# The keys' second parts in two zero-filled tiles, and the first gate's tile kept in DRAM meanwhile

## The chip, the core and the metric

The kernel runs on one NeuronCore of a Trainium2 chip. The metric is the device time of one execution in microseconds (us), lower is better. Before the change the median of three runs is 1441.95 us (1440.77 to 1442.16). About 0.2%, some 2.9 us, is what a measurement of this kernel can tell from no change.

## What is computed

One layer of a decoder block on 1024 tokens of width 1024, all in float32, with a first half (short convolution beside attention) and a gated MLP. The change lies in the attention's scores and in one of the gates. Cut to these:

```python
u = rmsnorm(x, norm_mix_w)
cb, cc, cx, q, k, v, g_conv, g_attn = split(u @ w_in + b_in)
q, k = rope(q), rope(k)            # 8 query heads, 2 key heads, 64 wide
# blocks of 128 queries against 256 keys: the block before and its own
scores = einsum('bnqhgd,bnkhd->bnhgqk', qb, kk) * 64 ** -0.5
probs  = softmax(scores with a window of 128 and a sink per head)
y_attn = (probs @ v) @ w_attn_out + b_attn_out
merged = sigmoid(g_conv) * y_conv + sigmoid(g_attn) * y_attn
```

## The kernel before

Products have float32 accuracy by splitting: a factor a is held as a first part `ah` (float32 rounded to the matmul's own type, fp32r) and a second part `al = a - ah`, and a product is the sum of three matmuls, `ah bh + ah bl + al bh` (`mm3`, lines 144 to 146). `split` (lines 138 and 139) makes the parts: a copy on ScalarE (ACT), then a subtraction on VectorE (DVE).

A head is 64 wide, half of the 128 rows that TensorE (PE) contracts over. So for each of the two key heads g the kernel packs both query parts into one 128-row operand: `qs[g]` holds the first parts of the queries in the head's own 64 rows (`own[g]`) and their second parts in the other 64 (`other[g]`). `ks[g]` holds the keys' first parts in both halves. One matmul of `qs[g]` with `ks[g]` over 128 rows (line 444) therefore gives two of the three products. The third one, first parts of the queries by second parts of the keys, is a matmul over the 64 rows `own[g]` alone (line 445), with `kl`: one tile, in which head 0 has the upper 64 rows and head 1 the lower.

The work is in 16 steps (`Step`, line 432), one for each pair of a query block n and a head g. The order on PE, ACT and DVE is written out by hand (`tc.manual_schedule`, lines 514 to 561). In step i, PE does the scores of step i+1 (8 matmuls of 256 columns, alternating lines 444 and 445), the eight transposes `pt` of step i's probabilities (line 473, `turn`), half of a gate's or conv input's projection (`fill_part`: 24 matmuls of 512 columns, lines 144 to 146, with `w_fill` as weights), and step i's product with the values (4 matmuls `o`, line 483). DVE takes the masked maximum of the new scores (line 451, `maxima`), sums head halves, makes the second part `pl` of the transposed probabilities, stores the step before, normalises (line 467, `norms`) and, in every second step, makes the second part of the next `w_fill` (line 139). ACT does the exponentials, the first parts and the evictions (`fill_evict`, line 430). Scores of step 0 stand in front of the loop, between the two halves of fill 1.

The fills 0 to 7 are the projections `g_attn`; they stay in SBUF as `gas = filled[:8]` (line 562) until the attention's output is projected. There, the sigmoid of each (line 789) multiplies the output projection `ya` (line 795), and POOL's queue writes the result to DRAM (`msp`, line 796). All these tiles, and `ks`, `kl`, `vs`, the probabilities' parts and the raw weights `rin` of the next stage, are taken from one pool, `act`, of 16 tiles of 128x1024 float32. A new tile waits until the one that held its place is no longer read.

Outside the hand-written stretches a scheduler sets the order: so in the transition behind the loop, where `raw_ao` and `rin` are loaded by SP's queue (lines 121 and 601), which issues strictly in order. The next stage's first parts (`pin`, line 627) and the last store of the loop (`qs`, line 138) then stand in one queue on ACT.

Of the kernel before, what the change touches and what calls it, by code (L numbers as in the profile page):

```python
# [9 lines left out]
F32 = mybir.dt.float32  # L10
F32R = mybir.dt.float32r
I32 = mybir.dt.int32
AF = mybir.ActivationFunctionType
ALU = mybir.AluOpType

P = 128
D = 1024
T = 1024
# [17 lines left out]
COL_BIN = 0  # L36
# [36 lines left out]
def hybrid_kernel(ctx, tc, x, pos, cst, pcol, norms, w_in, w_ao, w_co, w_mix, w_up, w_down, out):  # L73
    nc = tc.nc
# [6 lines left out]
    dram = ctx.enter_context(tc.tile_pool(name="dram", bufs=1, space=bass.MemoryType.DRAM))  # L81
# [9 lines left out]
    def act(name, dt=F32, shape=(P, T)):  # L91
        return actp.tile(list(shape), dt, name=name, tag="act")
# [4 lines left out]
    def mid(name, dt=F32, shape=(P, 4, T)):  # L97
        return midp.tile(list(shape), dt, name=name, tag="mid")

    def ps(name, shape=(P, T)):  # L100
        return psum.tile(list(shape), F32, name=name, tag="mm")
# [8 lines left out]
    def pc(i):  # L110
        return pcol_sb[:, i:i + 1]
# [12 lines left out]
    def split_unit(raw, name, spare=False, eng=None):  # L124
        if spare:
            hi, lo = act(f"wh_{name}", F32R), act(f"wl_{name}", F32R)
        else:
            hl = wp.tile([P, 2, 1024], F32R, name=f"w_{name}", tag="w")
            hi, lo = hl[:, 0], hl[:, 1]
        split(raw, hi, lo, eng)  # L130
        return hi, lo
# [4 lines left out]
    def split(src, hi, lo, eng=None):  # L136

        first = nc.scalar.copy(hi, src)
        (eng or nc.vector).tensor_sub(lo, src, hi.bitcast(F32))
        return first  # L140
# [46 lines left out]
    def gemm_part(acc, w, u, cols, kcs=range(KC)):  # L187
        for kc in kcs:
            f = slice(kc * P, (kc + 1) * P)
            mm3(acc[:, cols], w[0][:, f], w[1][:, f], u[:, 0, kc, cols], u[:, 1, kc, cols], kc == 0, kc == KC - 1)  # L190
# [177 lines left out]
    def rope(part):  # L368
        r, sw, name = part
        q = tmp(f"q_{name}")  # L370
        nc.vector.tensor_mul(q, r, cos)
        nc.vector.tensor_mul(sw, sw, sin)
        nc.vector.tensor_add(q, q, sw)
        return q
# [3 lines left out]
    own = [slice(0, HD), slice(HD, P)]  # L378
    other = [own[1], own[0]]
    qs = [mid(f"qs{g}", F32R) for g in range(2)]  # L380
    ks = [act(f"ks{g}", F32R) for g in range(2)]
    kl = act("kl", F32R)

    def rope_keys(part):
        k = rope(part)
        for g in range(2):
            split(k[own[g]], ks[g][own[g]], kl[own[g]])
        for g in range(2):
            nc.vector.tensor_copy(ks[g][other[g]], ks[g][own[g]].bitcast(F32))

# [8 lines left out]
    cos, sin = table_cos, table_sin  # L399
    ps_q2 = gemm_feat(w_q2, u, "q2")  # L400
    rope_keys(turn["k"])
    turn[2] = rope_load(ps_q2, COL_BIN + U_Q + 2, "q2")
    for i in range(2):
# [12 lines left out]
    filled = [None] * len(fillers)  # L416
    w_fill, ps_fill = {}, {}
# [4 lines left out]
    def fill_part(f, h, kcs):  # L422
        if h == 0 and kcs[0] == 0:
            ps_fill[f] = ps(f"ps_fill{f}")
        gemm_part(ps_fill[f], w_fill[f], u, halves[h], kcs)

    def fill_evict(f):
        col, alloc = fillers[f]
        filled[f] = alloc(f"fill{f}")
        return nc.scalar.activation(filled[f], ps_fill[f], AF.Identity, bias=pc(COL_BIN + col))  # L430

    class Step:
        def __init__(self, i):
# [2 lines left out]
            self.queries = slice(self.n * P, (self.n + 1) * P)  # L436

        def scores(self):
            rows, g = own[self.g], self.g
            w0 = max(0, self.n - 1) * P  # L440
            kc = slice(w0, w0 + 256)
            self.s = ps(f"s{self.name}", (P, 4, 256))
            for c in range(4):
                nc.tensor.matmul(self.s[:, c], qs[g][:, c, self.queries], ks[g][:, kc], start=True, stop=False)
                nc.tensor.matmul(self.s[:, c], qs[g][rows, c, self.queries], kl[rows, kc], start=False, stop=True)  # L445

        def maxima(self):
            self.p = tmp(f"p{self.name}", F32, (P, 4, 256))
# [65 lines left out]
    with tc.manual_schedule(engines={mybir.EngineType.PE, mybir.EngineType.Activation, mybir.EngineType.DVE}):  # L514
        st = [Step(i) for i in range(len(steps))]
        fill_part(1, 0, range(KC))
        st[0].scores()
        fill_evict(0)
        st[0].maxima()
        fill_part(1, 1, range(KC))  # L520
# [3 lines left out]
        for i, step in enumerate(st):  # L524
            nxt = st[i + 1] if i + 1 < len(st) else None
            prev = st[i - 1] if i else None
            f, h = 2 + i // 2, i % 2
# [4 lines left out]
            if h == 0:  # L532
                fill_evict(f - 1)
# [26 lines left out]
        after_attention = st[-1].store().ins  # L560
        wa.append(split_unit(raw_ao[1], "ao1"))
    gas = filled[:8]

# [210 lines left out]
    for q in range(4):  # L776
# [9 lines left out]
        for jj in range(2):  # L786
# [4 lines left out]
            for cols in halves:  # L791
                for c in range(4):
                    f = slice((jj * 4 + c) * P, (jj * 4 + c + 1) * P)
# [417 lines left out]
    with tc.manual_schedule(engines={mybir.EngineType.PE, mybir.EngineType.Activation, mybir.EngineType.DVE, mybir.EngineType.SP}):  # L1211
# [9 lines left out]
        for i in range(4):  # L1221
# [7 lines left out]
            else:  # L1229
                rows = slice(3 * P, 4 * P)  # L1230
# [89 lines left out]
```

## Time and profile before

| what | us |
|---|---|
| median of three runs | 1441.95 |
| the profiled execution | 1441.58 |
| its span, first to last instruction | 1439.8 |
| PE busy, share of the span | 1418.2 (98%) |
| DVE busy | 1003.6 (70%) |
| ACT busy | 562.5 (39%) |
| POOL busy | 85.7 (6%) |
| mean granted clock of TensorE | 0.997 of 2.4 GHz |

Busy time of PE is the time in which at least one matmul is in the array; matmuls overlap, so their durations don't add up to it, and the distance from one start to the next (the pitch) is what counts. PEld is the loading of a matmul's weights, which can overlap the matmul ahead. An idle time is followed in brackets by what ended it. The chain of work that ended last is followed back from the last instruction, each piece with the time that it adds.

### The profile page before, as it was taken

The page shows a single profiled execution, that of the slowest core. Times are in us where ns is not written, and L with a number is a line of the kernel's source. Part 1 is how long each engine was busy: PE and PEld are TensorE (multiplying, and loading weights), DVE is VectorE, ACT ScalarE, POOL GpSimd, SP SyncE. Part 2 cuts the span into 40 slices and gives each one's busy share as a digit, 9 for nine tenths or more (in the row PEclk, how much of TensorE's full clock was granted, in tenths as well). Part 3 has the DMA queues.
Part 4 walks back from the last instruction along what each step waited for, and adds up shares of the span by engine and source line. Part 5 has one row for each costly group of instructions (what it writes and reads, how often), then busy time and mean ns, then how long its engine had stood idle before and what let it go on. Part 6 is the DMA issues. An engine that isn't in the chain of part 4 may idle for free.

```text
span 1439.8 us, 17099 instructions
## 1 busy us (share of the span) xinstructions
PE 1418.2 (98%) x6447; PEld 1164.9 (81%) x6447; DVE 1003.6 (70%) x1511; ACT 562.5 (39%) x897; POOL 85.7 (6%) x144
## 2 busy tenths in 40 slices
PE   8999999999999999999999999999999999999997
PEld 6987777788888888877888878888888888888886
DVE  7575676856788787545644697787777777655567
ACT  5545555623333333232323543333333334444343
POOL 5210000000000000000000000000000000000000
PEclk9999999999999999999999999999999999999999
DMA  5320000242455554255552222222232225797603
GB/s 217 89 59 30 30 16 30 88 161 74 161 205 205 191 185 178 76 177 196 184 174 103 74 98 107 101 105 95 88 110 93 99 94 197 275 377 256 195 31 146
DMA packets 68450, 193.18 MB, mean 134 GB/s; under 512 B 8144, under 2 KB 8400, under 8 KB 68368
## 3 DMA queue, kind: packets, MB, share of 16 engines
q1 hardware_dynamic: 53280, 139.64, 28.8%
q0 software_dynamic: 14368, 51.13, 9.2%
q10 hardware_dynamic: 720, 1.33, 0.3%
q8 instruction: 50, 0.82, 0.2%
q14 instruction: 32, 0.26, 0.1%
HBM read 136.75 MB, written 52.69 MB: 132 GB/s over the span
## 4 chain that ended last, share of the span: by engine, by line
PE 86%; DVE 6%; DMA 5%; ACT 2%; issue 1%; SPq 0%; DVEq 0%; ACTq 0%
PE xup L649 8%; PE zup L649 8%; PE yup L649 8%; PE dna L1151 8%; PE dnb L1151 6%; PE yin L649 5%; PE xin L649 5%; PE zin L649 5%; PE wup L649 4%; PE win L649 3%; PE ps_fill L144 3%; PE ps_fill L146 3%; PE ps_fill L145 3%; PE mx L145 2%; PE mx L146 2%; PE mx L144 2%
## 5 line engine op out<-in xcount | busy, mean ns | idle before, releaser
L1138 DVE TENSOR_TENSOR pd<-rd,pd 128x1024 fp32r<-128x1024 f32 x77 | 93.7, 1222 | 54.1 <-ACT pd L1141 50.3
L627 ACT CAST pup<-sup 128x512 fp32r<-128x512 f32 x80 | 47.8, 620 | 203.2 <-DVE sup L613 203.2
L1141 ACT CAST pd<-rd 128x1024 fp32r<-128x1024 f32 x77 | 80.6, 1053 | 104.1 <-PE dnb L1151 37.1
L1151 PE MATMUL dna<-pd 128*128 128x512 f32 x528 | 120.3, 389 | 0.0
L1151 PEld LDWEIGHTS dna<-pd 128*128 128x128 f32 x528 | 99.1, 188 | 20.5
L1151 PE MATMUL dnb<-pd 128*128 128x512 f32 x396 | 90.2, 389 | 0.0
L1151 PEld LDWEIGHTS dnb<-pd 128*128 128x128 f32 x396 | 74.3, 188 | 15.4
L649 PE MATMUL zin<-u,pin 128*128 128x512 f32 x360 | 86.1, 389 | 0.0
L627 ACT CAST pin<-sin 128x512 fp32r<-128x512 f32 x52 | 31.1, 620 | 135.3 <-DVE sin L613 126.4
L649 PEld LDWEIGHTS zin<-u,pin 128*128 128x128 f32 x360 | 67.6, 188 | 14.0
L630 DVE TENSOR_TENSOR pup<-sup,pup 128x512 fp32r<-128x512 f32 x80 | 53.6, 689 | 18.5 <-ACT pup L627 15.0
L144 PE MATMUL ps_fill<-u,w_fill 128*128 128x512 f32 x160 | 64.0, 400 | 0.0
L146 PE MATMUL ps_fill<-u,w_fill 128*128 128x512 f32 x160 | 62.5, 391 | 0.0
L145 PE MATMUL ps_fill<-u,w_fill 128*128 128x512 f32 x160 | 62.3, 389 | 0.0
L649 PE MATMUL yup<-b22h,pup 128*128 128x512 f32 x176 | 57.9, 390 | 0.9 <-DVE aup L665 0.9
L649 PE MATMUL zup<-b11h,pup 128*128 128x512 f32 x176 | 57.8, 390 | 0.0
L649 PE MATMUL zup<-b21h,pup 128*128 128x512 f32 x176 | 57.7, 389 | 0.0
L451 DVE CUSTOM_DVE_ANT_0 p<-s,cst_sb,pcol_sb 128x256 f32<-128x256 f32 x64 | 27.2, 480 | 37.2 <-PE s L445 34.6
L649 PE MATMUL yup<-bt1h,pup 128*128 128x512 f32 x160 | 52.5, 389 | 0.0
L649 PE MATMUL wup<-bt2h,pup 128*128 128x512 f32 x160 | 52.5, 389 | 0.0
L649 PE MATMUL xup<-bt3h,pup 128*128 128x512 f32 x160 | 52.5, 389 | 0.0
L649 PE MATMUL xup<-bt4h,pup 128*128 128x512 f32 x160 | 52.5, 389 | 0.0
(361 smaller groups left out, 3470.4 us busy)
## 6 DMA issues: line engine op xcount, KB each, us to landing
rup<-in_w_up SPq DMA_DIRECT2D x44, 512.0 KB, 3.5
rin<-in_w_in SPq DMA_DIRECT2D x30, 512.0 KB, 6.7
td<-in_w_down SPq DMA_DIRECT2D x22, 512.0 KB, 5.3
tsp<-td POOLq DMA_DIRECT2D x22, 512.0 KB, 3.7
rd<-tsp SPq DMA_DIRECT2D x44, 256.0 KB, 5.3
rd<-in_w_down SPq DMA_DIRECT2D x33, 256.0 KB, 5.3
rd<-hs SPq DMA_DIRECT2D x33, 256.0 KB, 3.7
x<-in_x SPq DMA_DIRECT2D x16, 512.0 KB, 3.7
```

What stands on the lines that cost most here:

```text
L144: nc.tensor.matmul(dst, ah, bh, start=first, stop=False)
L145: nc.tensor.matmul(dst, ah, bl, start=False, stop=False)
L146: nc.tensor.matmul(dst, al, bh, start=False, stop=last)
L451: nc.vector.tensor_tensor_reduce(out=self.p[:, c], in0=self.s[:, c], in1=masks[0 if self.n == 0 else 1], scale=SCALE, scalar=pc(COL_SINK + ...
L627: nc.scalar.copy(self.parts[p, q][:, 0], src())
L630: v.tensor_sub(t[:, 1], src(), t[:, 0].bitcast(F32))
L649: nc.tensor.matmul(dst, a, b[:, kc], start=first and i == 0, stop=last and i == 2, skip_group_check=p >= PLAIN and more)
L1138: v.tensor_sub(t[:, 2:], raws_d[n - 1], t[:, :2].bitcast(F32))
L1141: nc.scalar.copy(parts_d[n][:, :2], raws_d[n])
L1151: nc.tensor.matmul(sets[side, i], t[:, s, tok], t[:, b], start=g == 0 and k == 0 and not more, stop=g == NG - 1 and k == 2, skip_group_che ...
```

## The change

The keys' second parts get a tile for each head, `kl[0]` and `kl[1]`. The half that doesn't belong to the head is set to zero by two memsets on POOL. The second matmul of each pair contracts over all 128 rows: the rows of the queries' second parts meet zeros, and the sum stays what it was.

The pool `act` still has 16 tiles, so one is given back: fill 0 is written to DRAM (`gsp0`) by POOL's queue as soon as it is evicted, its place is free, and it is loaded again as `ga0` behind the loop by SP's queue.

```diff
-    kl = act("kl", F32R)
+    kl = [act(f"kl{g}", F32R) for g in range(2)]
+    for g in range(2):
+        nc.gpsimd.memset(kl[g][other[g]].bitcast(F32), 0.0)
...
-            split(k[own[g]], ks[g][own[g]], kl[own[g]])
+            split(k[own[g]], ks[g][own[g]], kl[g][own[g]])
...
+    gsp0 = dram.tile([P, T], F32, name="gsp0")
+
     def fill_evict(f):
         col, alloc = fillers[f]
         filled[f] = alloc(f"fill{f}")
-        return nc.scalar.activation(filled[f], ps_fill[f], AF.Identity, bias=pc(COL_BIN + col))
+        nc.scalar.activation(filled[f], ps_fill[f], AF.Identity, bias=pc(COL_BIN + col))
+        if f == 0:
+            nc.gpsimd.dma_start(gsp0, filled[f])
...
         def scores(self):
-            rows, g = own[self.g], self.g
+            g = self.g
...
-                nc.tensor.matmul(self.s[:, c], qs[g][rows, c, self.queries], kl[rows, kc], start=False, stop=True)
+                nc.tensor.matmul(self.s[:, c], qs[g][:, c, self.queries], kl[g][:, kc], start=False, stop=True)
...
     gas = filled[:8]
+    gas[0] = act("ga0")
+    nc.sync.dma_start(gas[0], gsp0)
```

Lines of the changed kernel behind the last edit are 10 higher (line 601 is 611, line 795 is 805). PE's instructions stand in the same order as before.

SP's queue, behind the loop: `raw_ao` are weights of the output projection, `rin` of the next stage. Before:

```order
L121 DMA raw_ao1_2159<-in_w_ao 128x1024
L121 DMA raw_ao2_2420<-in_w_ao 128x1024
L601 DMA rin00_2506<-in_w_in 128x1024
L601 DMA rin01_2507<-in_w_in 128x1024
L121 DMA raw_ao3_2493<-in_w_ao 128x1024
```

And now:

```order
L121 DMA raw_ao1_2164<-in_w_ao 128x1024
L121 DMA raw_ao2_2427<-in_w_ao 128x1024
L572 DMA ga0_2305<-gsp0_948 128x1024
L611 DMA rin00_2513<-in_w_in 128x1024
L611 DMA rin01_2514<-in_w_in 128x1024
L121 DMA raw_ao3_2500<-in_w_ao 128x1024
```

The reload of the first gate stands between the third `raw_ao` and the two first `rin`.

DVE in the same place, at the products of the output projection `ya` with the gates; `ta`, `tb` and `tc` are sums for the next stage. Before:

```order
L741 TENSOR_TENSOR tb0_2429<-u1_94 128x1024
L795 SCALAR_TENSOR_TENSOR fill0_1056<-ya0_2309,pcol_sb_89,fill0_1056 128x1024
L742 TENSOR_TENSOR ta0_2425<-ta0_2425,tb0_2429 128x1024
L139 TENSOR_TENSOR w_ao2_2422<-raw_ao2_2420,w_ao2_2422 128x1024
L795 SCALAR_TENSOR_TENSOR fill1_1114<-ya1_2337,pcol_sb_89,fill1_1114 128x1024
L741 TENSOR_TENSOR tb1_2433<-u1_94 128x1024
L630 TENSOR_TENSOR pin02_2513<-rin01_2507,pin02_2513 128x512
```

And now:

```order
L751 TENSOR_TENSOR tb0_2436<-u1_94 128x1024
L752 TENSOR_TENSOR ta0_2432<-ta0_2432,tb0_2436 128x1024
L139 TENSOR_TENSOR w_ao2_2429<-raw_ao2_2427,w_ao2_2429 128x1024
L751 TENSOR_TENSOR tb1_2440<-u1_94 128x1024
L805 SCALAR_TENSOR_TENSOR ga0_2305<-ya0_2316,pcol_sb_89,ga0_2305 128x1024
L752 TENSOR_TENSOR ta1_2433<-ta1_2433,tb1_2440 128x1024
L805 SCALAR_TENSOR_TENSOR fill1_1119<-ya1_2344,pcol_sb_89,fill1_1119 128x1024
L640 TENSOR_TENSOR pin02_2520<-rin01_2514,pin02_2520 128x512
```

The first gate's product stands three instructions later, the second one's two.

POOL's queue, ahead of the attention; `sw` are the copies for the rotation of keys and queries. The piece of the difference, now:

```order
L223 TENSOR_TENSOR rt<-rt 128x256
L224 TENSOR_TENSOR rt<-rt 128x256
L385 MEMSET kl_708 64x1024
L385 MEMSET kl_709 64x1024
L365 DMA sw_k<-r_k 32x1024 x4
L365 DMA sw_q_720<-r_q_719 32x1024 x4
L365 DMA sw_q_727<-r_q_726 32x1024 x4
L365 DMA sw_q_793<-r_q_792 32x1024 x4
L365 DMA sw_q_870<-r_q_869 32x1024 x4
L438 DMA gsp_948<-fill_1060 128x1024
L806 DMA msp<-ga_2305 128x1024
```

The two memsets stand behind the rotation tables' last step and ahead of the keys' copies; the store of the first gate stands behind the last of those copies.

## Rows read from the trace of the kernel before

**Rows 1.** The page's part 4: shares of the chain that ended last, by engine

```profile
PE 86%; DVE 6%; DMA 5%; ACT 2%; issue 1%; SPq 0%; DVEq 0%; ACTq 0%
```

**Rows 2.** Stretches: length, busy time of PE, PEld, DVE, ACT, POOL, clock, DMA

```profile
137.00:146.70 9.70, 9.70 (x45) 7.48 (x44) 7.10 (x17) 4.67 (x13) 0.00 (x0) 1.00 0.15 54
263.40:270.70 7.30, 7.30 (x38) 6.19 (x37) 4.72 (x6) 3.17 (x4) 0.00 (x0) 1.00 0.15 43
```

**Rows 3.** PE in order of time, one step's scores: start, duration, engine, line

```profile
127.09 0.39 PE L483 MATMUL o<-pl,vs 128*128 128x512 f32 x1
127.32 0.28 PE L444 MATMUL s<-ks,qs 128*128 128x256 f32 x1
127.53 0.38 PE L445 MATMUL s<-kl,qs 64*128 64x256 f32 x1
...
129.71 1.09 PE L473 MATMUL pt<-cst_sb,p 128*128 128x128 f32 x8
```

**Rows 4.** The weight loads of the same two matmuls, in order of time

```profile
127.10 0.19 PEld L444 LDWEIGHTS s<-ks,qs 128*128 128x128 f32 x1
127.53 0.18 PEld L445 LDWEIGHTS s<-kl,qs 64*128 64x128 f32 x1 [0.24 <-issue]
```

**Rows 5.** The chain that ended last: start, time added, what

```profile
112.08 0.42 PE ps_fill L144
...
243.10 0.91 PE o L483 x4
...
246.30 1.02 PE pt L473 x8
...
262.52 0.91 PE o L483 x4
263.43 0.87 PE pt L473 x8
...
270.98 4.79 DMA rin<-in_w_in
...
316.12 5.44 PE xin L649 x24
```

**Rows 6.** The same chain, early: 256-column matmuls that are all 128 rows high

```profile
32.56 2.87 PE ps_q L288 x24
```

**Rows 7.** Weight loads of such matmuls, in order of time

```profile
57.82 1.87 PEld L288 LDWEIGHTS ps_q<-u,w_q 128*128 128x128 f32 x15
```

**Rows 8.** DVE in order of time, first and last work of two steps

```profile
129.82 0.48 DVE L451 CUSTOM_DVE_ANT_0 p<-s,cst_sb,pcol_sb 128x256 f32<-128x256 f32 x1 [3.86 <-PE s L445]
...
136.69 1.22 DVE L139 TENSOR_TENSOR w_fill<-raw_fill,w_fill 128x1024 fp32r<-128x1024 f32 x1
139.53 0.48 DVE L451 CUSTOM_DVE_ANT_0 p<-s,cst_sb,pcol_sb 128x256 f32<-128x256 f32 x1 [1.62 <-PE s L445]
...
145.50 1.22 DVE L467 TENSOR_TENSOR p<-p,sm 128x1024 f32<-128x1024 f32 x1
```

**Rows 9.** ACT in order of time, behind the loop

```profile
275.80 0.62 ACT L627 CAST pin<-rin 128x512 fp32r<-128x512 f32 x1 [3.40 <-DMA rin<-in_w_in]
276.44 0.61 ACT L138 CAST qs<-os 64x512 fp32r<-64x512 f32 x1
...
304.46 0.62 ACT L627 CAST pin<-rin 128x512 fp32r<-128x512 f32 x1 [1.34 <-DMA msp<-fill]
```

**Rows 10.** PE in order of time, behind the loop

```profile
277.11 0.73 PE L144 MATMUL ya<-qs,w_ao 128*128 128x512 f32 x2 [1.00 <-ACT qs L138]
```

**Rows 11.** Stretches behind the loop (columns as in Rows 2; the last is GB/s)

```profile
271.00:272.00 1.00, 1.00 (x6) 0.84 (x5) 1.00 (x2) 1.00 (x2) 0.00 (x0) 1.00 0.89 143
...
273.00:274.00 1.00, 1.00 (x6) 0.84 (x5) 1.00 (x2) 0.00 (x0) 0.00 (x0) 1.00 1.05 426
```

**Rows 12.** POOL in order of time, ahead of the attention

```profile
18.47 1.95 POOL L222 TENSOR_SCALAR rt<-rt 128x256 f32<-128x256 f32 x1
...
59.48 2.22 POOL L365 DMA_DIRECT2D sw_k<-r_k  x4 [20.91 <-ACT r_k L362]
```

## The prediction

> **What bounds the kernel now.** I read the chain of work that ended last first. 86% of it is PE [rows 1], so what PE is spared in a stretch where it doesn't wait comes off the end, unless something else is late there next. Then I read the attention loop by stretches: in a step of 9.70 us PE is busy for all 9.70, and so it is in the last step, which has no scores and takes 7.30 [rows 2]. So PE sets the loop's pace, and a step's scores cost about 2.4 us.
>
> Eight matmuls of 256 columns should not cost that. In time order, the first of them (128 rows) starts at 127.32, the second (64 rows) at 127.53, and the transposes behind the eighth start at 129.71 [rows 3]: the seven behind the first have (129.71 - 127.53) / 7 = 0.31 us each. The weight loads tell why. The load for the 128-row matmul at 127.32 started at 127.10, 0.22 us ahead of it, under a product of the values that is 128 rows high too. The load for the 64-row matmul starts at 127.53, together with its matmul, after an idle 0.24 that nothing in the profile explains but the issue itself [rows 4]. Where the height changes, the load is not pulled under the matmul ahead, and the heights alternate through all eight.
>
> Matmuls of the same 256 columns that all have 128 rows show the other case: 24 of them add 2.87 us to the chain, 0.12 each [rows 6], though each has its own load; 15 loads of some 0.19 take 1.87 together, so they overlap [rows 7].
>
> **The change, part by part.**
>
> *Scores over 128 rows.* From the chain: the values' product ends at 243.10 + 0.91 = 244.01, the transposes' turn begins at 246.30 and adds 1.02 [rows 5]. That is 2.29 for the eight, and the transposes carry a switch of height too: behind a 128-row matmul they add 0.87 (at 263.43, [rows 5]). Cost of a step's scores: 2.29 + 1.02 - 0.87 = 2.44. After: 8 x 0.12 = 0.96, with transposes at 0.87. Saved 1.48 in each of the 15 steps that hold scores, 22.2 in all. The scores in front of the loop are followed by a fill matmul that adds 0.42 [rows 5] where a steady 512-column matmul adds 5.44 / 24 = 0.23 [rows 5], so they save 2.29 - 0.96 + 0.19 = 1.52. Together 23.7 us. Bounds: the eight at the transposes' own pitch, 0.87 / 8 = 0.109, would save another 1.4; at no better than 0.31, nothing.
>
> *Does another engine take over at 9.71 - 1.48 = 8.23 us a step?* (9.71 is the distance between the two maxima in [rows 8].) In a step with a weight split DVE works from 129.82 to 136.69 + 1.22 = 137.91, 8.09 us; in the next from 139.53 to 146.72, 7.19 [rows 8]. Both fit, with 0.14 and 1.04 to spare, and the pair, 15.28 against 16.46, can't fall behind. The normalised probabilities are ready 7.19 after the maxima begin, and PE asks for them, 0.11 having passed before the maxima, at 8.12. ACT has less work than DVE in every stretch shown [rows 2]. So the loop stays PE's. For the scores ahead of the loop I show no such slack; if PE waits there for the first softmax, it loses at most the 1.52 saved there.
>
> *Two memsets of 64x1024 on POOL.* The trace has none. The nearest row is POOL's slowest on float32, 1.95 for 128x256 [rows 12]; four times that is 7.8 for one, 15.6 for both at the worst. POOL stands idle for 20.91 us ahead of the keys' copies [rows 12], which are queued behind them. So they cost nothing; what exceeded that idle time would delay the keys' rotation by as much.
>
> *Store of the first gate.* 512 KB to DRAM by POOL's queue, in a stretch in which DMA moves 54 GB/s [rows 2] and POOL has nothing else to issue. Nothing. It frees the 16th tile early in the loop, so the loop has as many tiles as before.
>
> *Reload of the first gate.* Here is a real price. Behind the loop PE waits 1.00 for the last stored queries [rows 10]; on ACT that copy (276.44) stands behind a `pin` copy that waited 3.40 for the second `rin` (275.80) [rows 9], whose load is 4.79 in the chain [rows 5]. The reload is now issued ahead of both `rin` in the same queue, so whatever it delays them by is added to PE's wait. Lower bound 0: all of its transfer could fit into time in which DMA isn't full ahead of `rin`. Upper bound: a whole landing, 4.79. Between: 512 KB (524 kB) at 426 GB/s are 1.23 us, and the us ahead of `rin`'s transfer had (426 - 143) GB/s free, 283 kB or 0.66 us [rows 11]. I take 0.57, nearest to the bytes' own row.
>
> *DVE's new order there.* The first gate's product comes three instructions later, some 3.7 us at 1.2 each, and with it the free tile for a `rin` of the second unit. Its `pin` copies end at 304.46 + 0.62 [rows 9], and PE starts the next stage at 316.12 [rows 5], 11 us later. Hidden; beyond 11 us each us would count.
>
> *Behind that* PE has the same instructions in the same order, and everything shifts with it.
>
> Sum on the profiled execution: 1441.58 - 23.7 + 0.57 = 1418.4. Its span is 1439.8 with 1.78 around it, and it lies 0.37 under the median, so the runs should show **1418.8**.
>
> **The rivals.**
>
> *Loads don't overlap after all (the saving fails).* If a load of the full height may not run under a full-height matmul, the pitch stays at 0.31, and only the reload's 0.57 is left: 1442.5. Against it speak the load at 127.10 [rows 4] and the 0.12 pitch [rows 6, 7]; for it, only that a pair here uses the same weights twice, which no row shows. The Trainium skill, "TensorE: Matmul & The Clock Gate", Part 3, says that weight loads overlap matmuls in flight only when their row groups differ. By that rule all 128-row loads would collide, and this rival would hold; the trace disagrees with it, with 15 loads in 1.87 us. 3%.
>
> *Half the saving.* The loads no longer overlap each other, and each matmul costs one load, 0.19: 1.52 a step, saved 0.92 x 15 + 0.96 = 14.8, time 1427.7. The 0.12 of the same form speaks against it. 6%.
>
> *DVE becomes the bound.* If DVE's 8.09, the hand-over of 0.11 and the transposes' 0.87 came in series in every step, it would last 9.07 and save 0.64: 1441.95 - 15 x 0.64 - 1.52 + 0.57 = 1431.4. It needs DVE's chain to pass 8.23; 0.14 is close in one step of two, but the next gives 1.04 back. 4%.
>
> *Slower.* The reload sits at the head of SP's queue behind the loop, and its whole landing goes into the wait of ACT's `pin` copy and so of PE: +4.79. With the saving that is 1422.8; it decides the sign only where the pitch stays as well: 1446.7. The idle share of DMA ahead of `rin` [rows 11] speaks against it. 2%.
>
> **How the numbers follow.** Forecast 85%. Its low end: the faster pitch (1.4) and no price for the reload (0.57) give 1416.8, less 0.8 for the spread of runs, 1416.0. Its high end: the reload's full 4.79 instead of 0.57, 1423.0, and the first scores' 1.52 lost, 1424.5. Beyond lie half the saving, DVE's bound and the two cases without one, 15%. Faster by over 0.2% (2.9 us, what a measurement can tell): forecast, half and DVE's bound, 95%. Same: 3%. Slower: 2%.
>
> **What would show it.** Right: the second score matmul has a load 128 rows high that starts ahead of its matmul; scores' pitch near 0.12, the transposes 0.87 in the chain, steps of 8.2 us with PE busy throughout; DVE's idle time ahead of the maxima down to about 0.1 in one step of two; PE's wait for the last queries behind the loop 1.0 to 2.5. Wrong: a pitch above 0.15, an idle time of PE in the loop that ends on DVE or ACT, a `rin` landing several us later, or keys' copies that POOL issues later than 59.5.

## The result and the profile after

The changed kernel takes 1421.12 us, the median of four runs (1419.90 to 1423.16), against 1441.75 for the kernel before beside it: a ratio of 0.9859, 95% interval 0.9842 to 0.9876, some 20.6 us less. The forecast was 1418.8, its range 1416.0 to 1424.5: the sign and the size held, and the point lay 2.3 us too low. The profiled execution took 1423.16 us, with a span of 1421.4, 18.4 less than before. That difference divides, by the starts and ends of PE's matmuls, into four parts:

| stretch | before | after | difference |
|---|---|---|---|
| start of the program to the end of the last `o` | 270.66 | 247.39 | -23.27 |
| from there to the first `xin` product | 45.30 | 49.49 | +4.19 |
| from there to the first `xup` product | 477.62 | 478.38 | +0.76 |
| from there to the end | 646.22 | 646.14 | -0.08 |

**The loop.** PE in order of time, one step's scores, answering to [rows 3]:

```profile
133.04 0.39 PE L491 MATMUL o<-pl,vs 128*128 128x512 f32 x1
133.27 0.28 PE L452 MATMUL s<-ks,qs 128*128 128x256 f32 x1
133.38 0.28 PE L453 MATMUL s<-kl,qs 128*128 128x256 f32 x1
133.50 0.28 PE L452 MATMUL s<-ks,qs 128*128 128x256 f32 x1
...
134.22 1.04 PE L481 MATMUL pt<-cst_sb,p 128*128 128x128 f32 x8
```

The weight loads of the first two of them, answering to [rows 4]:

```profile
133.05 0.19 PEld L452 LDWEIGHTS s<-ks,qs 128*128 128x128 f32 x1
133.27 0.19 PEld L453 LDWEIGHTS s<-kl,qs 128*128 128x128 f32 x1
```

The second matmul's load now starts at 133.27, ahead of its matmul (133.38) and together with the matmul before it; in [rows 4] it started with its own. From one matmul to the next pass 0.11 to 0.12 us, where it was 0.31 behind the first.

The chain of work that ended last (start, time added, what), answering to [rows 5] and, with its first line, [rows 6]:

```profile
33.37 2.87 PE ps_q L288 x24
...
126.16 0.87 PE pt L481 x8
...
132.53 0.91 PE o L491 x4
134.38 0.87 PE pt L481 x8
...
246.48 0.92 PE o L491 x4
...
247.69 6.56 DMA rin<-in_w_in
...
254.27 0.62 ACT pin L637
...
254.91 0.62 ACT qs L138
...
255.58 1.86 PE ya L144 x3
257.44 0.43 PE ya L145
```

The values end at 132.53 + 0.91 = 133.44 and the transposes begin at 134.38: the eight score matmuls take 0.94 (before: 2.29), and the transposes 0.87 (before: 1.02). A step is 134.38 - 126.16 = 8.22 long.

By stretches (length, busy time of PE, PEld, DVE, ACT, POOL, clock, DMA share, GB/s), that step, answering to [rows 2], and then the time behind the loop:

```profile
126.16:134.38 8.22, 8.22 (x47) 7.08 (x45) 7.24 (x17) 6.24 (x14) 0.00 (x0) 1.00 0.01 3
...
252.00:254.00 2.00, 0.83 (x4) 0.37 (x2) 1.94 (x3) 0.00 (x0) 0.00 (x0) 1.00 0.25 100
254.00:256.00 2.00, 0.42 (x1) 0.42 (x2) 1.44 (x3) 1.68 (x3) 0.00 (x0) 0.78 0.00 0
256.00:258.00 2.00, 2.00 (x5) 1.24 (x5) 1.97 (x3) 1.97 (x3) 0.00 (x0) 0.50 0.00 0
258.00:260.00 2.00, 2.00 (x6) 1.52 (x5) 1.97 (x3) 2.00 (x3) 0.00 (x0) 0.50 0.16 20
260.00:262.00 2.00, 2.00 (x7) 1.52 (x6) 1.18 (x1) 2.00 (x3) 0.00 (x0) 0.52 0.67 242
262.00:264.00 2.00, 2.00 (x10) 1.63 (x9) 1.23 (x2) 2.00 (x3) 0.00 (x0) 1.00 0.00 0
```

PE is busy for all of the step. DVE in order of time, the split of the weights and the first maximum of two steps, answering to [rows 8]:

```profile
133.07 1.22 DVE L139 TENSOR_TENSOR w_fill<-raw_fill,w_fill 128x1024 fp32r<-128x1024 f32 x1
134.42 0.48 DVE L459 CUSTOM_DVE_ANT_0 p<-s,cst_sb,pcol_sb 128x256 f32<-128x256 f32 x1
...
142.62 0.48 DVE L459 CUSTOM_DVE_ANT_0 p<-s,cst_sb,pcol_sb 128x256 f32<-128x256 f32 x1 [1.01 <-PE s L453]
```

In one step of two the split ends at 133.07 + 1.22 = 134.29, 0.13 ahead of the maximum at 134.42, and no wait is named there; in the other DVE waits 1.01 for PE. DVE is close to its bound, but not late.

**Behind the loop.** Here the 4.19 us were lost. ACT in order of time, answering to [rows 9]:

```profile
254.27 0.62 ACT L637 CAST pin<-rin 128x512 fp32r<-128x512 f32 x1 [5.15 <-DMA rin<-in_w_in]
254.91 0.61 ACT L138 CAST qs<-os 64x512 fp32r<-64x512 f32 x1
```

PE in order of time, answering to [rows 10]:

```profile
255.58 1.86 PE L144 MATMUL ya<-qs,w_ao 128*128 128x512 f32 x3 [2.75 <-ACT qs L138]
```

ACT waits 5.15 for `rin` (before: 3.40), and PE 2.75 for the copy behind it (before: 1.00). Then something new follows, in the stretches above: from 254 to 262 the granted clock is 0.50 to 0.78. Before the change it was 1.00 behind the wait:

```profile
278.00:280.00 2.00, 1.82 (x8) 1.50 (x9) 1.94 (x3) 1.97 (x3) 0.00 (x0) 1.00 0.00 0
```

At 0.50, which is TensorE's lower level of 1.2 GHz, the chain shows 0.43 for a matmul of 512 columns in place of 0.23.

**POOL**, answering to [rows 12]:

```profile
39.44 1.95 POOL L385 MEMSET kl<- 64x1024 f32 x2
60.28 1.74 POOL L365 DMA_DIRECT2D sw_k<-r_k  x3 [18.89 <-ACT r_k L362]
```

The two memsets take 1.95 together and end 18.89 us before POOL's next work.

### The profile page after: what moved, and what is told of

Same layout as the page of the kernel before. It is cut to its first block, busy times and chain, and to the rows that moved or that the text cites. A ratio compares the mean times of both kernels' runs of the same rounds, so it can differ in the third digit from the quotient of the medians.

```text
span 1421.4 us, 17106 instructions
## 1 busy us (share of the span) xinstructions
PE 1397.7 (98%) x6447; PEld 1161.5 (82%) x6447; DVE 1003.1 (71%) x1511; ACT 563.4 (40%) x897; POOL 88.1 (6%) x147
## 3 DMA queue, kind: packets, MB, share of 16 engines
q10 hardware_dynamic: 720, 1.33, 0.3%
## 4 chain that ended last, share of the span: by engine, by line
PE 87%; DVE 5%; DMA 5%; ACT 2%; issue 1%; SPq 0%; DVEq 0%; ACTq 0%
PE xup L659 8%; PE zup L659 8%; PE yup L659 8%; PE dna L1161 8%; PE dnb L1161 6%; PE yin L659 5%; PE xin L659 5%; PE zin L659 5%; PE wup L659 4%; PE win L659 3%; PE ps_fill L144 3%; PE ps_fill L146 3%; PE ps_fill L145 3%; PE mx L145 2%; PE mx L146 2%; PE mx L144 2%
## 5 line engine op out<-in xcount | busy, mean ns | idle before, releaser
L1161 PEld LDWEIGHTS dna<-pd 128*128 128x128 f32 x528 | 99.1, 188 | 20.6
L144 PE MATMUL yc<-z,co 128*128 128x512 f32 x128 | 48.3, 399 | 4.5 <-ACT co L138 2.6
```

What stands on the lines that cost most here:

```text
L144: nc.tensor.matmul(dst, ah, bh, start=first, stop=False)
L1161: nc.tensor.matmul(sets[side, i], t[:, s, tok], t[:, b], start=g == 0 and k == 0 and not more, stop=g == NG - 1 and k == 2, skip_group_che ...
```

## The experiments

Theory: each change of height costs PE some 0.19 us, so that the loop gains 24 us, and the reload delays `rin`, the copies on ACT and PE, and through PE's wait the clock. Rivals: 64-row matmuls are slow in themselves; the loss behind the loop comes with the faster loop; the clock falls for another reason.

The loss is best seen in two pieces of the stretch behind the loop: from the last `o` to the first product that needs the last queries (the wait lies in it), and from there to the first `xin` product (the same matmuls in every kernel). All starts and ends are PE's:

| kernel | last `o` ends | product with last queries | piece 1 | first `xin` | piece 2 |
|---|---|---|---|---|---|
| before | 270.66 | 277.11 | 6.45 | 315.96 | 38.85 |
| after | 247.39 | 255.58 | 8.19 | 296.88 | 41.30 |
| e1, reload only | 270.57 | 278.25 | 7.68 | 317.08 | 38.83 |
| e2, 128 rows only | 246.53 | 253.46 | 6.93 | 292.28 | 38.82 |
| e3, two changes of height | 253.62 | 260.00 | 6.38 | 298.86 | 38.86 |
| e4, copies later | 246.54 | 252.92 | 6.38 | 291.75 | 38.83 |
| e5, after again | 246.73 | 254.35 | 7.62 | 294.50 | 40.15 |
| e6, wait filled | 246.49 | 254.19 | 7.70 | 292.88 | 38.69 |
| e7, other gate | 246.57 | 253.23 | 6.66 | 292.07 | 38.84 |
| e8, sums later | 246.46 | no wait | - | 289.81 | 43.35 in all |

**e1: the reload alone**, in the kernel before.

```diff
-        return nc.scalar.activation(filled[f], ps_fill[f], AF.Identity, bias=pc(COL_BIN + col))
+        nc.scalar.activation(filled[f], ps_fill[f], AF.Identity, bias=pc(COL_BIN + col))
+        if f == 0:
+            nc.gpsimd.dma_start(gsp0, filled[f])
...
     gas = filled[:8]
+    gas[0] = act("ga0")
+    nc.sync.dma_start(gas[0], gsp0)
```

> The kernel before, with only the first gate's tile written to DRAM and read back after the attention; the scores stay as they were, with products over 64 rows. Theory (the loss of 4.2 us between the last values and the next weights' first product comes from the reload, which makes the next weights land later): steps of 9.7 us as before, that stretch 1 to 4.2 us longer than 45.44 us, median 1442.8 to 1446.0 us. Rival (the loss comes from the faster loop, not from the reload): stretch 45.4 us, median 1441.4 to 1442.2 us.

Measured: 1443.42 us (1441.89 to 1446.30, 11 runs) beside 1441.09, ratio 1.0018, interval 1.0009 to 1.0028. ACT, PE, and a stretch of e1:

```profile
276.94 0.62 ACT L633 CAST pin<-rin 128x512 fp32r<-128x512 f32 x1 [4.70 <-DMA rin<-in_w_in]
...
278.25 0.73 PE L144 MATMUL ya<-qs,w_ao 128*128 128x512 f32 x2 [2.24 <-ACT qs L138]
...
280.00:286.00 6.00, 6.00 (x28) 4.96 (x27) 4.36 (x5) 5.99 (x7) 0.00 (x0) 1.00 0.25 87
```

In this execution the reload made piece 1 longer by 1.23 us, at a clock that stayed at 1.00. The theory holds; the reload has a price with the old loop too. The runs up to 1446 leave room for executions in which more was lost. The clock may be the cause there: the five runs with a mean granted clock of 0.993 or 0.994 took 1443.42 to 1446.30 us, the six with 0.995 to 0.998 took 1441.89 to 1443.70. Where in those runs it was lower isn't shown.

What DMA did ahead of `rin`, first in the kernel before, then in e1 (the last figure is GB/s):

```profile
270.00:272.00 2.00, 2.00 (x10) 1.65 (x10) 2.00 (x2) 1.24 (x2) 0.00 (x0) 1.00 0.88 244
270.00:272.00 2.00, 2.00 (x11) 1.65 (x10) 2.00 (x2) 1.40 (x2) 0.00 (x0) 1.00 0.95 381
```

So DMA moved more in this stretch with the reload, and `rin` came later all the same.

**e2: 128 rows alone**, without reload.

```diff
-                nc.tensor.matmul(self.s[:, c], qs[g][rows, c, self.queries], kl[rows, kc], start=False, stop=True)
+                nc.tensor.matmul(self.s[:, c], qs[g][:, c, self.queries], kl[:, kc], start=False, stop=True)
```

> The kernel before, with the product with the second parts over all 128 rows, but with the one tile of second parts that both key heads share and no rows of zeros: the scores take up the query's second parts times the other head's second parts, which the reference does not have. No reload. Theory: steps of 8.2 us and scores of 0.96 us as after the change, the stretch behind the attention as before (45.4 us), median 1417.2 to 1418.5 us (1441.8 less 24.1). Rival (the loss behind the attention comes with the faster loop): median 1420.5 to 1421.5 us.

Measured: 1417.38 us (1416.88 to 1419.98), ratio 0.9840, interval 0.9826 to 0.9853: 23.7 us saved beside 1441.09, as the theory says. The last `o` ends 24.13 earlier than before. Piece 1 is 0.48 longer than before, since `rin` lands that much later behind the last `o`, with no reload ahead of it. So part of the longer wait comes with the faster loop; why stays open.

**e3: 64 rows, with two changes of height in a step.**

```diff
-            for c in range(4):
-                nc.tensor.matmul(self.s[:, c], qs[g][:, c, self.queries], ks[g][:, kc], start=True, stop=False)
-                nc.tensor.matmul(self.s[:, c], qs[g][rows, c, self.queries], kl[rows, kc], start=False, stop=True)
+            first = lambda c, start: nc.tensor.matmul(self.s[:, c], qs[g][:, c, self.queries], ks[g][:, kc], start=start, stop=not start)
+            second = lambda c, start: nc.tensor.matmul(self.s[:, c], qs[g][rows, c, self.queries], kl[rows, kc], start=start, stop=not start)
+            for c in (0, 2):
+                first(c, True)
+            for c in (0, 2):
+                second(c, False)
+            for c in (1, 3):
+                second(c, True)
+            for c in (1, 3):
+                first(c, False)
```

> The kernel before, with products over 64 rows kept, but put in the order 128, 128, 64, 64, 64, 64, 128, 128 rows (two changes of height in a step where there were eight). No other tile, no reload. Theory (the time goes at each change of height, 1.48 us a step over eight changes, 0.185 us each): 0.37 us a step left, scores of about 1.3 us, saved 1.11 us times 16 = 17.8, median 1424.0 us (1422.5 to 1426.5). Rival (a 64-row product is slow in itself, 0.37 us more than one of 128 rows): nothing saved, 1441.8 us; a fixed part of each: between, and the row of the scores says how it divides.

Measured: 1422.72 us (1422.35 to 1424.18), ratio 0.9875, interval 0.9862 to 0.9889, 18.4 us saved. The chain of e3, one step's scores:

```profile
133.90 0.91 PE o L490 x4
134.81 0.23 PE s L443 x2
135.04 0.66 PE s L444 x4
135.70 0.44 PE s L443 x2
136.14 0.87 PE pt L480 x8
```

The scores take 136.14 - 134.81 = 1.33, with four 64-row matmuls still among them. No change of height gives 0.94 (after), two give 1.33, eight gave 2.29, and 0.15 more in the transposes: (1.33 - 0.94) / 2 = 0.20 and (2.44 - 0.94) / 8 = 0.19 for each. The four 64-row matmuls add 0.66 together, too little for 0.31 each. So the time goes with the changes of height, and the 64-row matmul is not slow in itself.

**e4: ACT's copies of the next weights behind the last queries**, in the kernel after.

```diff
-            pin.prep(0, 3)
-            pin.prep(0, 2)
+            with tc.issue_after(after_attention):
+                pin.prep(0, 3)
+                pin.prep(0, 2)
```

> The kernel after the change, with ACT's two copies of the next weights' first parts put behind its copy of the last queries (they stood ahead of it and waited for the load). Theory (the PE's wait of 2.75 us for that copy let the clock fall to half, and cost about 1 us of wait and 3.2 us of half clock): the wait is about 1 us, the last queries being ready when VectorE's last sum is (0.2 to 0.4 us behind 253.07), granted clock 1.00 between 255 and 262 us, median 1416.8 to 1418.5 us. Rival (the clock falls after any such wait, or the load itself holds the PE up elsewhere): 1420.3 to 1421.5 us.

Measured: 1416.17 us (1416.09 to 1417.18), ratio 0.9829, interval 0.9816 to 0.9843. ACT and PE of e4:

```profile
252.25 0.62 ACT L138 CAST qs<-os 64x512 fp32r<-64x512 f32 x1 [3.98 <-DVE os L503]
...
252.92 0.73 PE L144 MATMUL ya<-qs,w_ao 128*128 128x512 f32 x2 [0.94 <-ACT qs L138]
```

The copy of the queries no longer stands behind one that waits for `rin`; it waits for DVE instead. Piece 1 is back at 6.38 and piece 2 at 38.83, with the reload still there: the theory holds, and the time is a little better than expected.

**e5: the kernel after once more.** No edit.

> The kernel after the change once more, to tell whether the fall of the clock behind the attention is the rule. Theory (it falls in most executions, and costs about 2.4 us net there): median 1420 to 1422 us, and the granted clock between 256 and 262 us is again about 0.5, or the time of the profiled execution is about 1418.5 us. Rival (the fall was one execution's): granted clock 1.00 there, and the median still 1420 to 1422 us, so that the 2.4 us must lie elsewhere.

Measured: 1419.44 us (1418.96 to 1424.64), ratio 0.9859, interval 0.9844 to 0.9874; the lower edge of what was expected was 1420. PE and stretches of e5:

```profile
254.35 0.85 PE L144 MATMUL ya<-qs,w_ao 128*128 128x512 f32 x2 [2.18 <-ACT qs L138]
...
254.00:256.00 2.00, 1.42 (x3) 0.80 (x4) 1.94 (x3) 1.96 (x3) 0.00 (x0) 0.70 0.00 0
256.00:258.00 2.00, 2.00 (x6) 1.61 (x5) 2.00 (x3) 1.99 (x3) 0.00 (x0) 0.50 0.00 0
258.00:260.00 2.00, 2.00 (x9) 1.60 (x9) 1.92 (x2) 2.00 (x3) 0.00 (x0) 0.95 0.70 162
```

The clock fell in this execution too, for a shorter time. The profiled execution took 1419.64, between the 1418.5 expected without a fall and the first one's 1423.16.

**e6: the wait filled with products of zeros**, in the kernel after.

```diff
+                for n, (i, cols) in enumerate(order):
+                    if q == 0 and n == 2:
+                        with tc.issue_after(last.ins):
+                            for _ in range(N_FILL):
+                                nc.tensor.matmul(yas[0][:, cols], zero[:, :P], zero, start=True, stop=True)
```

(`N_FILL` is 12. `order` holds the halves of `ya0` and `ya1` in the order that PE already had; `last` is the last product ahead of the wait.)

> The kernel after the change, with twelve products of zeros (128x512, 0.227 us each, 2.7 us in all) put on TensorE where it waits 2.75 us for the last queries; the next product clears what they wrote, so the sums are unchanged. Theory (the idle time makes the clock fall): the queries come at the same time (no gain in the wait itself), the granted clock stays at 1.00, median 1418.7 us (1418.0 to 1419.4). Rival (the clock falls there for another reason than the idle time): granted clock again about 0.5 for six microseconds, median 1420.3 to 1422.5 us.

Measured: 1418.82 us (1417.50 to 1419.93), ratio 0.9846, interval 0.9833 to 0.9860. PE and stretches of e6:

```profile
252.00 2.54 PE L808 MATMUL ya<-zero 128*128 128x512 bf16 x11
254.19 1.43 PE L145 MATMUL ya<-qs,w_ao 128*128 128x512 f32 x3
...
254.00:256.00 2.00, 1.89 (x9) 1.18 (x8) 1.94 (x3) 1.97 (x2) 0.00 (x0) 1.00 0.00 0
256.00:258.00 2.00, 2.00 (x11) 1.63 (x10) 2.00 (x3) 1.99 (x3) 0.00 (x0) 1.00 0.00 0
```

Piece 1 is as in e5 (7.70 and 7.62): the queries came no sooner. But the clock stayed at 1.00, and piece 2 is 38.69 in place of 40.15 and 41.30. Counted against e6, the fall cost 1.46 us in e5 and 2.61 in the first execution. This is what the theory says, that the idle time brings the fall, but it rests on one traced execution with the wait filled, and in e1 a wait of 2.24 was followed by no fall. The medians, 1418.82 and 1419.44, lie too close together to decide it.

**e7: another gate in DRAM**, the seventh, read back behind the loads of `rin`.

```diff
-        if f == 0:
+        if f == 6:
             nc.gpsimd.dma_start(gsp0, filled[f])
...
-    gas[0] = act("ga0")
-    nc.sync.dma_start(gas[0], gsp0)
...
             pin.load(0)
+            gas[6] = act("ga6")
+            nc.sync.dma_start(gas[6], gsp0)
             pin.prep(0, 3)
```

> The kernel after the change, with the seventh gate's tile in DRAM in place of the first's, read back behind the loads of the next weights on the same queue. Theory (0.5 MB of reload ahead of those loads is what made them land 1.2 us later): TensorE's wait is about 1.5 us as without a reload (253.46 less 251.97), the clock does not fall, median 1417.5 us (1417.0 to 1418.6). Rival (a reload costs the same wherever it stands, since it now keeps other loads or the seventh gate's product waiting): 1419.8 to 1421.8 us.

Measured: 1417.17 us (1416.66 to 1417.50), ratio 0.9835, interval 0.9821 to 0.9848. ACT and PE of e7:

```profile
251.91 0.62 ACT L635 CAST pin<-rin 128x512 fp32r<-128x512 f32 x1 [3.62 <-DMA rin<-in_w_in]
...
253.23 0.73 PE L144 MATMUL ya<-qs,w_ao 128*128 128x512 f32 x2 [1.22 <-ACT qs L138]
```

With the same bytes behind `rin`, PE waits 1.22, and piece 2 is 38.84. What cost was the reload's place ahead of `rin`.

**e8: DVE's sums later too**, on top of e4. DVE's four sums for the next product stood ahead of the last sum of the attention; here they follow the last queries' second parts.

```diff
+            self.second = nc.vector.tensor_sub(lo, self.os[r], hi.bitcast(F32))
...
-            next(gen_in)
-            next(gen_in)
+            with tc.issue_after(st[-1].second.ins):
+                next(gen_in)
+                next(gen_in)
```

> The kernel with ACT's two copies of the next weights behind the last queries, as in the run of 1416.17 us, and also VectorE's four sums of 1.1 us for the next product behind the last queries' second parts. Theory (the wait that is left, 0.94 us and 0.34 us and some 0.4 us of modelled tails, comes from the last sum standing behind those four): TensorE has no wait between the last values and the next weights' first product, median 1414.6 us (1414.0 to 1415.4). Rival (the four sums, later by some 2 us, then hold up the gates' products or the next weights): 1416 to 1418 us.

Measured: 1415.89 us (1413.20 to 1416.83), ratio 0.9823, interval 0.9809 to 0.9836; 1.3 us above what was expected. DVE, ACT and PE of e8:

```profile
247.16 0.69 DVE L503 TENSOR_TENSOR os<-o,os 64x512 f32<-64x512 f32 x1 [0.29 <-ACT os L499]
...
248.21 0.62 ACT L508 CAST qs<-os 64x512 fp32r<-64x512 f32 x1
...
251.73 0.84 PE L144 MATMUL ya<-qs,w_ao 128*128 128x512 f32 x3
```

The last queries' first parts are ready at 248.21 + 0.62 = 248.83, three us before PE asks for them at 251.73, and PE no longer waits. The stretch is 43.35, 1.86 less than in e4 (45.21). But the middle stretch, from there to the first `xup`, was 478.15 against 476.48 in e4, so that in these two executions nearly all was given back. Whether that is a rule was the next question.

**e9 and e10: e4 and e8 again, on one chip.** No edits.

> The kernel with ACT's two copies behind the last queries once more, beside the next run on the same chip: median 1416.2 us (1415.8 to 1417.0), stretch between the last values and the first xin product 45.2 us, middle stretch from there to the first xup product 476.5 to 477.5 us.

> The kernel with VectorE's four sums behind the last queries too, once more: its first stretch was 43.35 us, 1.86 us shorter than with the copies alone, and its middle stretch 478.15 us, 1.67 us longer. Theory (the gain is given back, since the middle stretch waits for loads that do not come earlier): middle stretch again 1 us or more longer than in the run beside it, median within 0.6 us of that run's. Rival (the longer middle stretch was that execution's chance): middle stretches alike, median 1.3 to 2.0 us below that run's, 1414.2 to 1414.9 us.

Measured: e9 1417.53 us (1417.20 to 1419.32), ratio 0.9834 (0.9820 to 0.9847); e10 1415.93 (1414.99 to 1416.56), ratio 0.9820 (0.9806 to 0.9833), beside 1441.79 for the kernel before. The stretches behind the loop are 45.24 and 43.36, the middle ones 477.56 and 477.60. So the theory fails, the longer middle stretch did not come back in this pair, and the difference of 1.60 us lies within the rival's 1.3 to 2.0; both medians lay above what was expected, by some 1 us. The middle stretch varies by more than 2 us over the traced executions (475.82 in e3, 478.38 in the first after). That this is chance alone isn't shown: the three with DVE's sums later (478.15, 477.60 and, in e11, 478.08) lie above all others but that first one.

**e11: e10 with the seventh gate in DRAM**, as in e7.

> As the run before, with the seventh gate's tile in DRAM in place of the first's, read back behind the next weights' loads. Theory (TensorE has no wait left that the reload could lengthen): the same as the run before, within 0.5 us. Rival (the weights that now land 1.2 us earlier let the later loads and the middle stretch start earlier): 0.6 to 1.5 us below it.

Measured: 1416.03 us (1414.90 to 1417.90), ratio 0.9825 (0.9811 to 0.9838), stretch behind the loop 43.36: the same as e10. Without a wait of PE, the place of the reload has no price that these runs can tell.

The version with both edits of e8 is faster than both kernels: 1415.89 us on the chip on which the kernel after took 1419.44 and the one before 1440.97.

## Why the prediction was right, and where it was off

- **Scores: right.** Predicted were 0.96 for the eight, transposes at 0.87, steps of 8.2 and 23.7 us saved; the rows show 0.94, 0.87 and 8.22. The last `o` ends 24.1 earlier than before in e2 and e4 (270.66 to 246.53 and 246.54). The reason given, a load that is not pulled under a matmul of another height, is borne out by e3, where the 64-row matmuls stay and three quarters of the changes go.
- **The rule that spoke against it.** The Trainium skill, "TensorE: Matmul & The Clock Gate", Part 3, lists that weight loads overlap a matmul in flight only when their row groups differ. The trace after disagrees: the load at 133.27 runs beside the matmul that starts at 133.27, both over 128 rows. The prediction left out that the same part of the Trainium skill also lets a load into the background weight buffer be pulled ahead; the trace doesn't show which buffer a load goes to. The rival (1442.5) and the half saving (1427.7) fall with the pitch of 0.12.
- **DVE as the bound: it isn't, by little.** The forecast left it 0.14 in one step of two and 1.04 in the other; the rows after show 0.13 and 1.01, and PE stays busy through the step.
- **Memsets, store, DVE's new order: nothing, as said.** The two memsets took 1.95 together where the bound was 15.6. The trace before did have one on POOL, of 128x512 in bfloat16 at 0.52 us, a nearer row than the one that was used. POOL's key copies came 0.8 later than the 59.5 named as a sign of error, but 18.89 us behind the memsets, on the end of ACT's `r_k`: that execution started late by as much, and the other execution of the same code did not (59.61 in e5; below).
- **The reload: this term was too small, and its working failed.** The forecast took 0.57 us, the bytes at full rate (1.23) less 0.66 for free bandwidth ahead of `rin`. e1 measured 1.23 in piece 1. Beside e2, which has the faster loop and no reload, piece 1 was 0.69 longer in e5 and 1.26 in the first execution. That e1's figure equals the bytes' time doesn't show that nothing came off it: DMA did move more ahead of `rin` (381 GB/s from 270 to 272 in e1, 244 before), and yet `rin` came later by the 1.23. The term took the free room from the GB/s alone; by the DMA share of the same row in [rows 11], 0.89, little of that us was idle. What sets the delay stays open. "Whatever it delays them by is added to PE's wait" was right, and e4 and e7 show it from both sides.
- **Two terms that were missing.** In e2 the faster loop alone made piece 1 0.48 longer. And the forecast priced the wait at its own length, without the clock: in e5, counted against e6, a wait of 2.18 us cost 1.46 more behind it, and in the first execution one of 2.75 cost 2.61. With 0.4 more from the loop, 0.6 more in piece 1 and 1.5 to 2.6 for the clock, the forecast becomes 1418.8 - 0.4 + 0.6 + 1.5 to 2.6 = 1420.5 to 1421.6; measured were 1421.12 and 1419.44. This sum is made afterwards, from a few traced executions, and leaves the second median outside. e6, in whose trace the clock did not fall, took 1418.82.
- **What was luck.** The range held the measured time, but its upper end stood for a whole landing of the reload (4.79) and the first scores' 1.52 lost. Neither came; the fall of the clock, which the range wasn't made for, took part of that room.
- **The rest of the profiled execution.** It lost 0.81 at the start (the chain's first `ps_q` after 32 us began at 33.37 against 32.56 in [rows 6]) and 0.76 in the middle stretch. The late start goes with the clock: over the first 20 us its granted clock was 0.91, and so it was in e3 and e10, the two others that started late (33.63 and 33.51); in all other traced executions it was 0.98 or 1.00. The middle stretch varies as told under e10. e5, the same code, shows neither loss, so neither is put down to the change.

## What to carry to other kernels

Where matmuls of different heights alternate, the change of height costs more than the rows that it spares: pad with zeros, or put matmuls of one height together, which alone saved 18.4 us here, where full height saved 23.7 (e2), and needs no memory. Before a load is put at the head of a queue, look for what waits for the loads behind it, and which engine's queue that waiting instruction blocks; here moving the blocking copies (e4, 1416.17 us; e9, 1417.53) and moving the load (e7, 1417.17) did about equally well, and with DVE's sums moved too (e8) it was 1415.89, on the chip of e7. Price a new wait of PE together with the stretch behind it, since the clock can fall there.

## What the runs showed of the hardware

- A change between 64 and 128 rows costs about 0.19 us in these steps: 0.20 by two changes in a step (e3), 0.19 by eight (before). In e3's chain, at 0.94 / 8 = 0.1175 for each matmul, it is 0.19 going down (0.66 for four) and 0.21 coming up (0.44 for two).
- Idle times of nearly the same length ended differently: 2.18 us were followed by a granted clock of 0.50 (e5), 2.24 by 1.00 (e1). Filled with products of zeros, a time of the same length left it at 1.00 (e6). So the length of the idle time alone doesn't decide; what else does is open.
- The time at the lower level differed as well: PE's matmuls were slow from 254.35 to about 258 in e5, from 255.58 to about 262 in the first execution.
- Two memsets of 64x1024 float32 on POOL took 1.95 us together, as long as the one subtraction of a constant from 128x256 in [rows 12].
